# A decoder layer's MLP: up- and down-projection weights fetched, summed and split one k pair at a time, and further ahead

## The chip, the cores and the metric

One core of a Trainium2 chip runs the whole layer in one launch. The metric is device time in microseconds (us). TensorE (PE) multiplies, VectorE (DVE), ScalarE (ACT) and GpSimd (POOL) do element-wise work, SyncE (SP) issues DMAs. Each engine takes its instructions in order, in the order that the kernel's scheduler has written out.

## The reference, cut to what matters

The layer is a hybrid decoder block on 1024 tokens of width 1024: three kinds of attention, gates, an output projection, and then the MLP, which is what the change touches:

```python
h2 = rms_norm(x, norm_mlp_g[l])
x = x + jnp.square(jax.nn.relu(h2 @ w_up[l])) @ w_down[l]      # 1024 -> 4096 -> 1024, float32
```

## The kernel before

Float32 products are made from halves: an operand is split into a rounded `hi` and a remainder `lo` (`split`, ScalarE copies at L90, VectorE subtracts at L91), and each product is three matmuls (`mm3`, L75): hi hi, hi lo, lo hi. The MLP's two big products use a seven-product scheme for 2 x 2 blocks (`PROD`): seven products of sums of blocks instead of eight of blocks. So each step of one k pair (two blocks of 128 along the contraction) is 7 x 3 = 21 matmuls of 128x512, and each run of the loop collects seven PSUM banks, `p0` to `p6`, out of eight. The next run's second product needs a bank of the run before, so evacuation has to follow at once.

**Up-projection (`wino`, 64 steps).** The input `xo` (four k pairs, X0 to X3) stays in SBUF. Runs go over 16 groups of columns, u = 0 to 15, four steps each, but the first group is cut in two, because its last two inputs aren't there yet: u0 with k pairs 0 and 1, u1 whole, u0 with k pairs 2 and 3, then u2 to u15. Per pair of k pairs, `wino_w` has one DMA of 512 KB (SP) into one of two buffers, four GpSimd instructions of 128x256 (`wino_s`, L1105 to L1108) that make the sums of blocks, and then per k pair one split into one of four `wo` buffers. `ahead()` calls it once per step, before the step's matmuls. When a run ends, the banks are combined into four tiles `u2, c11, u3, c21` (L1173 to L1180: one copy on ScalarE, seven adds on VectorE). `use_up` multiplies these by the norm (L1323, VectorE), takes relu and square (L1324, L1325, ScalarE), and makes the sums of blocks for the next product (`wino_t`, L1085 to L1088, `xts`, three on VectorE and one on GpSimd). Squares and sums are stored to DRAM as `r_d` by two DMAs on SP (L1327, L1328).

The norm's own statistics are worked out in between (`rstd`, called through `first`: a few small matmuls `px`, and copies such as L1348).

**Down-projection (64 steps, 16 passes of four).** Pass p makes column group p mod 4 from input k pairs q = p to p + 3. X[q] is loaded from `r_d` (`xload`, L1406, in two pieces, one of four buffers in three), split, and its buffer is used again by X[q + 4], which can load when the last reader of X[q] is done. Weights come per k pair (`wload`, L1413, 256 KB, four GpSimd instructions of 128x128, three `wo` buffers). After a pass the seven banks are added to accumulators (L1457 by ScalarE, L1459 by VectorE); in the first four passes x itself is loaded into some of these first (L1451, L1452). The last passes write the output (L1476 on).

What stands first in each engine's queue is set by a scheduler that works on these loops in program order, with priorities of its own; where `pinned` is set the matmuls' order is as written.

Of the kernel before, what the change touches and what calls it, by code (L numbers as in the profile page):

```python
# [10 lines left out]
F32 = mybir.dt.float32  # L11
# [6 lines left out]
P = 128  # L18
# [13 lines left out]
def f32(ap):  # L32
    return ap.bitcast(F32)
# [22 lines left out]

class Layer:
    def __init__(self, tc, a, out):
        self.tc, self.nc, self.a, self.out = tc, tc.nc, a, out
        self.n = 0  # L60
# [22 lines left out]
    def po_tile(self):  # L83
        return self.ptp.tile([P, 512], F32, tag="tp", name=self.name("po"))

# [995 lines left out]
    def wino_t(self, b):  # L1081

        V, G = self.nc.vector, self.nc.gpsimd
# [4 lines left out]
        V.tensor_sub(t[:, 3], b[:, 3], t[:, 1])  # L1088
# [11 lines left out]
    nwr = nwo = -1  # L1100
# [9 lines left out]
    def wino_w(self, src, kp):  # L1110

        nc = self.nc
        if kp % 2 == 0:
            self.nwr += 1
            self.wraw = self.wrp[self.nwr % 2].tile([P, 2, 8, P], F32, tag="wraw", name=self.name("wraw"))
            nc.sync.dma_start(self.wraw[:, :, 0:4], src[:, kp : kp + 2])
            r = self.wraw
            self.wino_s(r.rearrange("p k q n -> p q k n"))
        r = self.wraw[:, kp % 2]
        self.nwo += 1  # L1120
        wo = self.wop[self.nwo % 4].tile([P, 7, 2, P], F32R, tag="wo", name=self.name("wo"))
        self.split(wo[:, :, 0], wo[:, :, 1], r[:, 1:8])
        return wo

    def wino(self, ws, load, use, first, parts):


        nc = self.nc
        V = nc.vector
# [3 lines left out]
        plan = iter([(u, kp) for u, kps in runs for kp in kps])  # L1133
        W, X = {}, {}

        def ahead():
            n = next(plan, None)
            if n is not None:
                W[n] = self.wino_w(ws[n[0]], n[1])

        ahead()
        for kp in range(3):
            X[kp] = self.wino_x(kp, load)
            if kp == 0:
                ahead()
        for r, (u, kps) in enumerate(runs):
            bank = lambda j: f"p{(7 * r + j + 4) % 8}"
            ps = [self.pw.tile([P, 512], F32, tag=bank(j), name=self.name(f"p{j}")) for j in range(7)]
            for kp in kps:
                ahead()  # L1150
                if (r, kp) == (1, 0):
                    X[3] = self.wino_x(3, load)
                w, x = W[u, kp], X[kp]
                for j, (l, q) in enumerate(self.PROD):
                    self.mm3(ps[j], (w[:, l, 0], w[:, l, 1]), (x[:, q, 0], x[:, q, 1]), kp == kps[0], kp == kps[-1])
                    if (r, kp, j) in ((0, 1, 1), (1, 1, 6), (1, 2, 6), (1, 3, 3)):
                        first(bank(7))
            if r == 0:
                part = parts()
                for t, m in zip(part, ps):  # L1160
                    nc.scalar.copy(t, m)
                continue
            tl = lambda n: self.ev.tile([P, 512], F32, tag=n, name=self.name(n))
            u2, c11, u3, c21 = (tl(n) for n in ("u2", "c11", "u3", "c21"))
            if r == 2:
                for t, m in zip(part, ps):
                    V.tensor_add(t, t, m)
                m1, m2, m6, m7, m4, m5, m3 = part
                V.tensor_add(c11, m1, m2)
                V.tensor_add(u2, m1, m6)  # L1170
            else:
                m1, m2, m6, m7, m4, m5, m3 = ps
                nc.scalar.copy(u2, m1)  # L1173
                V.tensor_add(c11, u2, m2)
                V.tensor_add(u2, u2, m6)  # L1175
            V.tensor_add(u3, u2, m7)
            V.tensor_add(c21, u3, m4)
            V.tensor_add(u3, u3, m5)
            V.tensor_add(u2, u2, m5)
            V.tensor_add(u2, u2, m3)  # L1180
            use(u, (u2, c11, u3, c21))
        self.nwino = len(runs)
        self.pinned = False
# [35 lines left out]
    def tail(self):  # L1219
# [11 lines left out]
        with ExitStack() as c0:  # L1231
# [67 lines left out]
            with ExitStack() as c1:  # L1299
                E = lambda *x, **k: c1.enter_context(tc.tile_pool(*x, **k))  # L1300
                one_ = lambda n: E(name=n, bufs=1)
                xo2, xo3, wrp2, self.ev, wop1, self.xtp, self.xrp, xo0, xo1, wrp1 = (
                    one_(n) for n in ("xo2", "xo3", "wrp2", "ev", "wop1", "xtp", "xrp", "xo0", "xo1", "wrp1")
# [3 lines left out]
                self.wrp, self.wop = (wrp1, wrp2), (wop1, *wop2)  # L1307
# [10 lines left out]
                def use_up(u, cs):  # L1318

                    b = self.xrp.tile([P, 4, 512], F32, tag="xr", name=self.name("rq"))  # L1320
                    for i in (1, 3, 2, 0):
                        hf = i % 2
                        V.tensor_mul(cs[i], cs[i], rb[:, hf * 512 : (hf + 1) * 512])  # L1323
                        nc.scalar.activation(cs[i], cs[i], AF.Relu)  # L1324
                        nc.scalar.activation(b[:, i], cs[i], AF.Square)  # L1325
                    t = self.wino_t(b)
                    nc.sync.dma_start(self.rd[u, :, 0:3], b[:, 1:4])  # L1327
                    nc.sync.dma_start(self.rd[u, :, 3:7], t)  # L1328

# [34 lines left out]
    def down(self):  # L1364
# [4 lines left out]
        with ExitStack() as c1:  # L1369
# [30 lines left out]
            def xload(q):  # L1400

                out = []
                for pool, i, n in xp[q % 4]:
                    t = pool.tile([P, n, 2, 512], F32R, tag=f"x{i}", name=self.name("xd"))
                    raw = f32(t[:, :, 1])
                    nc.sync.dma_start(raw, self.rd[kp(q), :, i : i + n])  # L1406
                    self.split(t[:, :, 0], t[:, :, 1], raw)
                    out += [(t[:, j, 0], t[:, j, 1]) for j in range(n)]
                return out

            def wload(g, kp):
                r = wr.tile([P, 8, P], F32, tag="wraw", name=self.name("wraw"))
                nc.sync.dma_start(r[:, 0:4], a["wdown"][g][:, kp])  # L1413
                self.wino_s(r)
                w = wo.tile([P, 7, 2, P], F32R, tag="wo", name=self.name("wo"))
                self.split(w[:, :, 0], w[:, :, 1], r[:, 1:8])
                return [(w[:, j, 0], w[:, j, 1]) for j in range(7)]

            self.pinned = True
            X = {}  # L1420
            passes = [(p % 4, tuple(range(p, 4 + p))) for p in range(16)]
            last = len(passes) - 1

            W = {}
            plan = iter([(p, q) for p, (g, qs) in enumerate(passes) for q in qs])

            def ahead():
                n = next(plan, None)
                if n is not None:
                    W[n] = wload(n[0] % 4, kp(n[1]))  # L1430

            ahead()
            ahead()
            for p, (g, qs) in enumerate(passes):
                A = acc[g]
                ps = [
# [3 lines left out]
                for run in (qs[0:1], qs[1:2], qs[2:4]) if p == last else [(q,) for q in qs]:  # L1440
                    for q in run:
                        if q not in X:
                            X[q] = xload(q)
                        ahead()
                    for j, (l, x) in enumerate(self.PROD):
                        for q in run:
                            self.mm3(ps[j], W[p, q][l], X[q][x], q == qs[0], q == qs[-1])
                if p < 4:
# [5 lines left out]
                if p <= last - 4:  # L1454
                    for j in range(7):
                        if p < 4 and j in (0, 2, 3):
                            nc.scalar.copy(A[j], ps[j])  # L1457
                        else:
                            V.tensor_add(A[j], A[j], ps[j])  # L1459
                    if p == last - 4:  # L1460
# [13 lines left out]
                if p < last:  # L1474
                    for j in range(7):
                        add(A[j], A[j], ps[j])  # L1476
                    add(a2, a2, a1)
# [10 lines left out]
                else:  # L1488

                    m1, m2, m6, m7, m4, m5, m3 = ps  # L1490
                    nc.scalar.copy(a1, m1)
# [166 lines left out]
```

## Time and profile before

| | us |
|---|---|
| median of 3 runs | 2282.09 (2279.72 to 2284.4) |
| the profiled execution | 2282.35, its span 2280.5 |
| up-projection, first matmul (`p<-xo,wo`) | 1639.42 |
| down-projection, first matmul (`p<-xd,wo`) | 1958.73 |
| last matmul row's start, 37 matmuls | 2267.78 |
| PE, DVE, ACT, POOL busy in the whole span | 96%, 60%, 44%, 21% |
| mean granted TensorE clock | 0.992 |

Times in the profile are microseconds from the span's start. A row of an engine's timeline has start, duration, engine, line, operation, `out<-in`, shape and count; in square brackets is the time for which the engine was idle ahead of it, and who ended that. A slice row has its window, its length, the busy time of PE, PEld (weight loads), DVE, ACT and POOL with the count of instructions in it, the granted TensorE clock, the DMA engines' share and GB/s. A group row has busy time and mean nanoseconds of one instruction, then idle time ahead of it.

### The profile page before, as it was taken

To read this page: it belongs to the slowest core of one execution; us is meant where nothing else is said; L and a number is where in the kernel's file an instruction comes from. 1 tells how busy PE (TensorE), PEld (TensorE's weight loads), DVE (VectorE), ACT (ScalarE), POOL (GpSimd) and SP (SyncE) were. 2 spreads that over 40 slices of the span, in tenths; PEclk is the share of its full clock that TensorE was granted. 3 is DMA by queue.
4 is the path that set the end of the run, shared out by engine and by line. 5 is a ranking of instruction groups with operands and counts; after the bars stand their busy time and mean duration, and the time that the engine had idled before them with its cause. 6 is when DMAs were issued, how large, how long until landed. Compare 5 with 4: busy or idle time off the path is not lost.

```text
span 2280.5 us, 30318 instructions
## 1 busy us (share of the span) xinstructions
PE 2193.9 (96%) x11222; PEld 1878.6 (82%) x11222; DVE 1376.1 (60%) x2627; ACT 1011.8 (44%) x1994; POOL 482.9 (21%) x568
## 2 busy tenths in 40 slices
PE   7999899999999999999898999999999999999999
PEld 5788789887899899999787888887777888778887
DVE  6635457552147877777662124453588777966678
ACT  6533445543246666666553102223444444543332
POOL 2100000000011101111000002101444444665553
PEclk9999999999999999999999999999999999999999
DMA  6023212201321110111135225434644444754444
GB/s 243 24 80 98 86 45 80 84 28 56 98 65 33 38 29 22 31 38 33 33 115 174 91 96 180 134 106 162 203 133 163 152 153 153 280 189 146 151 157 167
DMA packets 113268, 247.89 MB, mean 109 GB/s; under 512 B 10553, under 2 KB 19038, under 8 KB 111070
## 3 DMA queue, kind: packets, MB, share of 16 engines
q1 hardware_dynamic: 113118, 245.94, 32.8%
q8 instruction: 88, 1.44, 0.3%
q14 instruction: 62, 0.51, 0.1%
HBM read 178.76 MB, written 67.14 MB: 108 GB/s over the span
## 4 chain that ended last, share of the span: by engine, by line
PE 70%; DVE 12%; DMA 8%; ACT 5%; issue 3%; POOL 1%; SPq 0%; DVEq 0%; ACTq 0%; POOLq 0%
PE mm L75 41%; PE p L75 19%; PE sc L75 5%; PE po L75 2%; PE tp L78 2%; DMA raw<-in_wd 1%; DVE w L91 1%; ACT dpe L966 1%; DMA xd<-r_d 1%; DVE sc L958 1%; DMA raw<-in_wgate 1%; DVE wo L91 1%; DVE dpe L979 1%; PE pr L78 1%; DVE daT L91 1%
## 5 line engine op out<-in xcount | busy, mean ns | idle before, releaser
L75 PE MATMUL mm<-w,hT 128*128 128x384 f32 (+3 forms) x2496 | 474.2, 331 | 13.8 <-DVE dq L846 9.1
L75 PE MATMUL mm<-hT,w 128*128 128x512 f32 x1920 | 466.9, 397 | 10.7 <-ACT w L90 8.0
L75 PEld LDWEIGHTS mm<-hT,w 128*128 128x128 f32 x1920 | 355.8, 189 | 87.5 <-ACT w L90 9.9
L75 PEld LDWEIGHTS mm<-w,hT 128*128 128x128 f32 x2496 | 387.4, 189 | 33.7 <-DVE dq L846 13.8
L75 PE MATMUL p<-xd,wo 128*128 128x512 f32 x1344 | 309.7, 392 | 8.0 <-DVE xd L91 5.2
L75 PE MATMUL p<-xo,wo 128*128 128x512 f32 x1344 | 308.9, 391 | 6.0 <-DVE u L1175 3.2
L75 PEld LDWEIGHTS p<-xd,wo 128*128 128x128 f32 x1344 | 254.1, 189 | 63.5 <-DVE xd L91 6.4
L75 PEld LDWEIGHTS p<-xo,wo 128*128 128x128 f32 x1344 | 252.4, 189 | 61.1 <-DVE u L1175 3.9
L91 DVE TENSOR_TENSOR w<-raw,w 128x256 fp32r<-128x256 f32 (+3 forms) x304 | 172.7, 589 | 165.4 <-ACT w L90 164.6
L75 PE MATMUL mm<-kt,w 128*128 128x512 f32 x1152 | 261.6, 389 | 0.4 <-DVE w L91 0.4
L75 PEld LDWEIGHTS mm<-kt,w 128*128 128x128 f32 x1152 | 216.1, 188 | 45.6 <-DVE w L91 0.8
L90 ACT CAST w<-raw 128x256 fp32r<-128x256 f32 (+3 forms) x304 | 154.1, 532 | 200.5 <-PE mm L75 110.5
L90 ACT CAST wo<-wraw 128x896 fp32r<-128x896 f32 x128 | 120.2, 941 | 222.1 <-POOL wraw L1108 104.3
L91 DVE TENSOR_TENSOR wo<-wraw,wo 128x896 fp32r<-128x896 f32 x128 | 147.4, 1155 | 82.4 <-ACT wo L90 82.3
L966 ACT ACTIVATE dpe<-sc,dst,drr 128x256 f32<-128x256 f32 (+7 forms) x128 | 106.8, 834 | 93.7 <-DVE dst L962 91.7
L1105 POOL TENSOR_TENSOR wraw<-wraw 128x128 f32<-128x128 f32 (+1 forms) x96 | 74.9, 780 | 219.2 <-DMA wraw<-in_wdown 110.3
L91 DVE TENSOR_TENSOR xd<-xd 128x1536 fp32r<-128x1536 f32 (+2 forms) x43 | 81.8, 1910 | 56.4 <-ACT xd L90 56.3
L958 DVE CUSTOM_DVE_ANT_0 sc<-sc,tmask 128x256 f32<-128x256 f32 (+7 forms) x128 | 97.0, 757 | 16.3 <-PE sc L75 16.3
L1108 POOL TENSOR_TENSOR wraw<-wraw 128x128 f32<-128x128 f32 (+1 forms) x96 | 90.9, 947 | 7.5
L90 ACT CAST xd<-xd 128x1536 fp32r<-128x1536 f32 (+2 forms) x43 | 65.0, 1519 | 60.2 <-DMA xd<-r_d 60.2
L106 POOL TENSOR_SCALAR drr<-drr 128x16 f32<-128x16 f32 x16 | 3.5, 220 | 397.8 <-DVE drr L914 397.8
L75 PE MATMUL mm<-mh,w 128*128 128x512 f32 x256 | 80.6, 395 | 3.8 <-DVE w L91 3.0
(312 smaller groups left out, 2970.9 us busy)
## 6 DMA issues: line engine op xcount, KB each, us to landing
wraw<-in_wup SPq DMA_DIRECT2D x32, 512.0 KB, 4.7
r_d<-xts SPq DMA_DIRECT2D x16, 1024.0 KB, 4.9
wraw<-in_wdown SPq DMA_DIRECT2D x64, 256.0 KB, 2.8
xd<-r_d SPq DMA_DIRECT2D x19, 768.0 KB, 6.1
xd<-r_d SPq DMA_DIRECT2D x14, 1024.0 KB, 5.4
raw<-in_wgate SPq DMA_DIRECT2D x48, 256.0 KB, 3.0
gates<-gt SPq DMA_DIRECT2D x48, 256.0 KB, 2.0
raw<-in_wd SPq DMA_DIRECT2D x32, 384.0 KB, 3.2
```

The costliest lines, as they stand in the source:

```text
L75: self.pin(self.nc.tensor.matmul(out, l, r, start=start, stop=stop))
L78: self.pin(self.nc.tensor.transpose(out, x, self.ident))
L90: nc.scalar.copy(hi, src)
L91: nc.vector.tensor_sub(lo, src, f32(hi))
L106: g.tensor_scalar(r, ss, 1.0 / width, EPS, op0=ALU.mult, op1=ALU.add)
L958: V.tensor_tensor_reduce(out=sc[:, 0:n], in0=sc[:, 0:n], in1=self.tmask[:, D - n : D], scale=1.0, scalar=-3.0e38, op0=ALU.add, op1=ALU.max ...
L966: nc.scalar.activation(pe[c][:, 0:n], sc[:, 0:n], AF.Exp, bias=t8[:, 2 + c : 3 + c], scale=rr[:, i, c : c + 1], accum_out=t8[:, 4 + c : 5 ...
L979: V.scalar_tensor_tensor(out=pe[0][:, 0:n], in0=pe[1][:, 0:n], scalar=t8[:, 7:8], in1=pe[0][:, 0:n], op0=ALU.mult, op1=ALU.add)
L1105: G.tensor_add(r[:, 4], r[:, 0], r[:, 3])
L1108: G.tensor_sub(r[:, 7], r[:, 2], r[:, 5])
```

## The change

- A shared helper `wino_steps` takes the place of `wino_w` and `wload`: per k pair one DMA of 256 KB into the next of its raw buffers (four in the up-projection, in the memory of the two pairs; three in the down-projection, as before) and four GpSimd sums of 128x128. `raw()` issues load and sums of the next k pair, `wsp(n)` splits the weight of a later step (three steps on in the up-projection, two in the down-projection) after step n's matmuls, and then calls `raw()`. The numbers of `wo` buffers stay.
- In the up-projection the first group's partial results are combined in place, and its relu, squares and sums are spread over later steps by generators (`whole`, `todo`). `use_up` is a generator too: squares first, `xts` a step later.
- The store of the squares (`r_d` 0:3) is issued by ScalarE's queue.
- In the down-projection, loads and splits of X are apart: `xdma(q)` after the last step that reads the buffer, `xsplit` of the first piece three steps ahead of first use and of the others two. `side(n)` does this after every step.
- `self.V` and `self.A` are VectorE and ScalarE themselves; the class `InOrder` is added and not used.

By instruction counts, GpSimd has 128 more (573 to 701), SP issues 32 more loads and 16 fewer stores, ScalarE issues 16 DMAs more; TensorE's and VectorE's counts are those of before.

```diff
+    def split2(self, hi, lo, src):
+
+        self.A.copy(hi, src)
+        self.V.tensor_sub(lo, src, f32(hi))
...
-    def wino_w(self, src, kp):
-
-        nc = self.nc
-        if kp % 2 == 0:
-            self.nwr += 1
-            self.wraw = self.wrp[self.nwr % 2].tile([P, 2, 8, P], F32, tag="wraw", name=self.name("wraw"))
-            nc.sync.dma_start(self.wraw[:, :, 0:4], src[:, kp : kp + 2])
-            r = self.wraw
-            self.wino_s(r.rearrange("p k q n -> p q k n"))
-        r = self.wraw[:, kp % 2]
-        self.nwo += 1
-        wo = self.wop[self.nwo % 4].tile([P, 7, 2, P], F32R, tag="wo", name=self.name("wo"))
-        self.split(wo[:, :, 0], wo[:, :, 1], r[:, 1:8])
-        return wo
+    def wino_steps(self, srcs, wrp, wop, lead):
+        raws, W = [], []
+
+        def raw():
+            n = len(raws)
+            if n < len(srcs):
+                r = wrp.tile([P, 8, P], F32, tag="wraw", name=self.name("wraw"))
+                self.nc.sync.dma_start(r[:, 0:4], srcs[n])
+                self.wino_s(r)
+                raws.append(r)
+
+        def wsp(n, split=self.split2, more=True):
+            m = len(W)
+            if m < len(srcs) and m <= n + lead:
+                wo = wop.tile([P, 7, 2, P], F32R, tag="wo", name=self.name("wo"))
+                split(wo[:, :, 0], wo[:, :, 1], raws[m][:, 1:8])
+                W.append(wo)
+            if more:
+                raw()
+
+        return raw, wsp, W
...
+        raw, wsp, W = self.wino_steps([ws[u][:, kp] for u, kps in runs for kp in kps], self.wrp, self.wop, 3)
...
+                if kp != kps[-1]:
+                    wsp(n)
+                    for f in todo.pop(n, []):
+                        next(f)
+            if r == 0:
+                part = parts()
+                for t, m in zip(part, ps):
+                    A.copy(t, m)
+                wsp(n)
+            elif r == 2:
+                for t, m in zip(part, ps):
+                    V.tensor_add(t, t, m)
+                wsp(n)
+
+                def whole():
+                    c = combine(part, False)
+                    yield
+                    yield from use(0, c)
+
+                next(late)
+                g = whole()
+                todo.update({n + 1: [late], n + 3: [g], n + 5: [g], n + 8: [g]})
+            else:
+                cs = combine(ps, True)
+                wsp(n)
+                g = use(u, cs)
...
                     for i in (1, 3, 2, 0):
                         hf = i % 2
-                        V.tensor_mul(cs[i], cs[i], rb[:, hf * 512 : (hf + 1) * 512])
-                        nc.scalar.activation(cs[i], cs[i], AF.Relu)
-                        nc.scalar.activation(b[:, i], cs[i], AF.Square)
-                    t = self.wino_t(b)
-                    nc.sync.dma_start(self.rd[u, :, 0:3], b[:, 1:4])
+                        self.V.tensor_mul(cs[i], cs[i], rb[:, hf * 512 : (hf + 1) * 512])
+                        self.A.activation(cs[i], cs[i], AF.Relu)
+                        self.A.activation(b[:, i], cs[i], AF.Square)
+                    self.A.dma_start(self.rd[u, :, 0:3], b[:, 1:4])
+                    yield
+                    t = self.wino_t(b, self.V)
                     nc.sync.dma_start(self.rd[u, :, 3:7], t)
+                    yield
...
+            raw, wsp, W = self.wino_steps([a["wdown"][g][:, kp(q)] for g, q in steps], wr, wo, 2)
...
+            def side(n):
+
+                wsp(n)
+                for q in use1:
+                    if q >= 4 and use9[q - 4] == n:
+                        xdma(q)
+                for q in use1:
+                    if q >= 3 and n == use1[q] - 3:
+                        xsplit(q, (0,))
+                    if q >= 3 and n == use1[q] - 2:
+                        xsplit(q, (1, 2))
```

More of the change, by code (lines that the diff above doesn't have):

```diff
@@ L1098, in wino_x @@
         return xo
-    nwr = nwo = -1
     def wino_s(self, r):
@@ L1125, in wino @@
     def wino(self, ws, load, use, first, parts):
-        nc = self.nc
-        V = nc.vector
+        V, A = self.V, self.A
         self.pinned = True
         runs = [(0, (0, 1)), (1, (0, 1, 2, 3)), (0, (2, 3))] + [(u, (0, 1, 2, 3)) for u in range(2, len(ws))]
[L1133 to L1175, printed above, removed]
@@ L1403, in xload, with xdma @@
+            def xdma(q):
+                X[q] = []
                 for pool, i, n in xp[q % 4]:
                     t = pool.tile([P, n, 2, 512], F32R, tag=f"x{i}", name=self.name("xd"))
[L1405 to L1433, printed above, removed]
+                    nc.sync.dma_start(f32(t[:, :, 1]), self.rd[kp(q), :, i : i + n])
```

124 lines of the change are left out of this document (105 added, 19 removed).

## The prediction

> **What bounds the kernel now.** I read the page first, then the slices of 10 us over the two stages that the change touches, TensorE's timeline in them, and the rows around each hole. The slices' sum (busy time from 1640 to 2280 us, mean in tenths) says which engine to watch:
>
> ```profile
> sum 640.00, PE 620.94 PEld 509.55 DVE 483.30 ACT 277.82 POOL 325.80; mean PE 9.70 PEld 7.96 DVE 7.55 ACT 4.34 POOL 5.09
> ```
>
> TensorE is busy 97% of it, so the change can only win back holes, or dig new ones. The change keeps every matmul. TensorE's timeline (start, duration, count, idle before and its releaser):
>
> ```profile
> 1652.53 14.53 PE L75 MATMUL p<-xo,wo 128*128 128x512 f32 x63 [1.58 <-ACT pt L1161]
> ...
> 1672.20 1.16 PE L75 MATMUL px<-dg,ones 128*128 128x128 f32 x8 [1.51 <-ACT rb L1348]
> ...
> 1709.21 22.00 PE L75 MATMUL p<-xo,wo 128*128 128x512 f32 x87 [3.18 <-DVE u L1175]
> 1734.06 224.83 PE L75 MATMUL p<-xo,wo 128*128 128x512 f32 x990 [0.43 <-DVE u L1179]
> 1958.73 6.86 PE L75 MATMUL p<-xd,wo 128*128 128x512 f32 x28
> 1967.65 5.05 PE L75 MATMUL p<-xd,wo 128*128 128x512 f32 x21 [2.06 <-DVE xd L91]
> 1975.87 49.48 PE L75 MATMUL p<-xd,wo 128*128 128x512 f32 x209 [3.16 <-DVE xd L91]
> 2027.18 239.70 PE L75 MATMUL p<-xd,wo 128*128 128x512 f32 x1049 [1.83 <-DVE acc L1459]
> ```
>
> Undisturbed, a matmul takes 224.83 / 990 = 0.2271 us, so one step (21 matmuls) 4.77 us and one run or pass of four steps 19.1 us. All holes lie in the first 95 us of the up-projection and the first 70 us of the down-projection. The slices (busy time and count of PE, PEld, DVE, ACT, POOL, then the clock) give each hole's whole price, with the slowed matmuls after it:
>
> ```profile
> 1670.00:1680.00 10.00, 8.49 (x42) 6.86 (x41) 7.64 (x11) 5.46 (x9) 4.39 (x5) 1.00 0.10 37
> ...
> 1700.00:1710.00 10.00, 6.82 (x30) 5.16 (x28) 7.42 (x9) 1.73 (x3) 8.92 (x9) 1.00 0.94 330
> 1710.00:1720.00 10.00, 9.86 (x37) 7.88 (x37) 8.47 (x12) 8.58 (x13) 1.50 (x2) 0.83 0.50 143
> ...
> 1730.00:1740.00 10.00, 8.90 (x37) 6.40 (x36) 9.02 (x13) 6.54 (x11) 5.04 (x5) 1.00 0.29 90
> ...
> 1970.00:1980.00 10.00, 6.84 (x23) 5.17 (x23) 10.00 (x8) 4.40 (x4) 9.46 (x7) 0.83 0.68 247
> ```
>
> A slice without a hole counts about 45 (44 that start in it, and edges). After the 3.18 us hole the granted clock is 0.83 for a slice, with 37 matmuls. Against 45, the slices from 1700 and 1710 lack 15 + 8 = 23 matmuls, 23 x 0.2271 = 5.2 us; the one from 1730 lacks 8, 1.8 us; the hole at 1672 is 1.5 us by its own row.
>
> **Why those holes are there.** The rows at the largest one, oldest first (a DMA from the chain of waits, then the engines' timelines), those at the other two, and the wait's total (us, times, longest):
>
> ```profile
> 1697.94 4.45 DMA wraw<-in_wup
> 1706.20 0.94 ACT L90 CAST wo<-wraw 128x896 fp32r<-128x896 f32 x1 [5.61 <-POOL wraw L1108]
> 1707.17 1.39 DVE L91 TENSOR_TENSOR wo<-wraw,wo 128x896 fp32r<-128x896 f32 x1 [2.51 <-ACT wo L90]
> 1708.48 0.67 DVE L1175 TENSOR_TENSOR u<-u,p 128x512 f32<-128x512 f32 x1
> 1726.74 0.94 ACT L90 CAST wo<-wraw 128x896 fp32r<-128x896 f32 x1 [6.17 <-POOL wraw L1108]
> 1670.72 0.94 ACT L90 CAST wo<-wraw 128x896 fp32r<-128x896 f32 x1 [7.35 <-POOL wraw L1108]
> ACT wo L90 <- POOL wraw L1108: 95.8, 25, 7.4
> ```
>
> A raw weight pair lands at 1702.4, GpSimd's sums (L1108 is the last) hold it further, ScalarE waits 5.61 us with the split of that weight at the head of its queue, VectorE waits behind it, and the evacuation of the finished banks (L1175) stands behind that split in VectorE's order. TensorE needs the bank. The other two holes have the same row in front, 6.17 and 7.35 us of ScalarE waiting for L1108; at 1672 it is the broadcast copy L1348 that queues behind it.
>
> **Part 1, raws per k pair.** The price of a load and of its sums (landing; GpSimd rows with count, busy and mean ns; the pair's form first):
>
> ```profile
> wraw<-in_wup SPq DMA_DIRECT2D x32, 512.0 KB, 4.7
> wraw<-in_wdown SPq DMA_DIRECT2D x64, 256.0 KB, 2.8
> L1105 POOL TENSOR_TENSOR wraw<-wraw 128x256 f32<-128x256 f32 x30 | 31.7, 1056 | 68.7 <-DMA wraw<-in_wup 56.9 <-DVE xts L1088 9.0 <-DVE c L1174 2.7
> L1107 POOL TENSOR_TENSOR wraw<-wraw 128x256 f32<-128x256 f32 x30 | 28.9, 962 | 0.0
> L1106 POOL TENSOR_TENSOR wraw<-wraw 128x256 f32<-128x256 f32 x30 | 25.6, 855 | 0.0
> L1108 POOL TENSOR_TENSOR wraw<-wraw 128x256 f32<-128x256 f32 x30 | 24.1, 802 | 2.4
> L1105 POOL TENSOR_TENSOR wraw<-wraw 128x128 f32<-128x128 f32 x64 | 41.5, 648 | 126.3 <-DMA wraw<-in_wdown 110.3 <-DVE wo L91 15.9
> L1107 POOL TENSOR_TENSOR wraw<-wraw 128x128 f32<-128x128 f32 x64 | 35.5, 555 | 0.0
> L1106 POOL TENSOR_TENSOR wraw<-wraw 128x128 f32<-128x128 f32 x64 | 46.6, 728 | 0.0
> L1108 POOL TENSOR_TENSOR wraw<-wraw 128x128 f32<-128x128 f32 x64 | 65.4, 1021 | 5.0
> ```
>
> Before, a pair's buffer is free when the split of the pair two back is done, and its own first split comes three steps later: 3 x 4.77 = 14.3 us, of which load (4.7) and sums (1.06 + 0.96 + 0.86 + 0.80 = 3.68) take 8.4. That leaves 5.9 us on paper, and any bunching of splits, or another DMA ahead in SP's queue, eats it. After, each of four slots is free four steps before its next split: 19.1 us, less 2.8 for the same 256 KB as in the down-projection and 0.65 + 0.56 + 0.73 + 1.02 = 2.95 for sums of that shape: 13.3 us of slack. SP's queue still holds raws behind the first loads of xd, whose 4.84 us is seen in this row; 13.3 - 4.8 is still 8.5:
>
> ```profile
> 1704.55 4.84 SPq L1406 DMA_DIRECT2D xd<-r_d  x2
> ```
>
> So the split heads no queue with its raw missing, and the three holes go: 1.5 + 5.2 + 1.8 = 8.5 us. I keep 0.5 of the last one, since VectorE is 90% busy in its slice as it is, and the spread of the first row's result now lands there: -8.0. From the other side, the bound is the part that is surely a raw's wait, 3.18 + 1.51 = 4.7; on the far side -10, with the hole of 1.58 us at 1652. That one I leave: its two raws are still issued there. In the order of the changed kernel ScalarE and VectorE are not pinned by the new helper class, which nothing instantiates; the order that the scheduler gives has the same evacuation, behind a split, in every steady run.
>
> What it adds: 32 more DMA issues on SP, and 128 more GpSimd instructions. GpSimd's sums in the up-projection go from 30 x 3.68 = 110 to 62 x 2.95 = 183 us of about 320; still under 60% of them, cost 0. But they run beside VectorE:
>
> ```profile
> 1960.37 0.46 POOL L1105 TENSOR_TENSOR wraw<-wraw 128x128 f32<-128x128 f32 x1 [6.43 <-DMA wraw<-in_wdown]
> 1974.06 2.08 POOL L1105 TENSOR_TENSOR wraw<-wraw 128x128 f32<-128x128 f32 x1 [0.38 <-DMA wraw<-in_wdown]
> 1972.47 3.35 DVE L91 TENSOR_TENSOR xd<-xd 128x2048 fp32r<-128x2048 f32 x1
> ```
>
> The same sum takes 0.46 us with VectorE out of the way and 2.08 us while VectorE splits a wide tile. The Trainium skill, "SBUF - State Buffer", section Who interferes with whom, says that GpSimd shares one port pair with VectorE under an exclusive lock; these rows agree, and by that rule more GpSimd instructions mean more chances to hold VectorE up, which speaks against the change. Priced from rows: if each of the 64 weight splits is held by one more free-running sum, 64 x 0.46 = 29 us of VectorE, 1.8 per run, against a VectorE that is 75.5% busy by the sum (4.7 us free per run): 0 on the path, except in the runs that are already full, where it is up to 2 x 1.8 = +3.6. I take 0 and put 3.6 in the range.
>
> **Part 2, squares stored from ScalarE's queue.** Sixteen issues move from SP. An SP issue takes 0.42 us in this row; if ScalarE pays the same, 0.42 per run of 19.1 us:
>
> ```profile
> 1698.41 0.42 SPq L1327 DMA_DIRECT2D r_d<-rq  x1
> ```
>
> ScalarE is about half idle, so 0; if its copies wait behind an issue, at most 16 x 0.42 = +6.7 spread over runs whose evacuations have slack, of which I count +1 as the outer bound. What SP gains is nothing that a wait showed.
>
> **Part 3, the change of stage, 1958 to 1986.** VectorE is the bound there (10.00 busy in the slice above); its work is not made less. X1's and X2's wide splits ended the two TensorE holes of 2.06 and 3.16 us. What moves: X0's last third loads earlier, and X4's split goes ahead of the evacuation of the first pass:
>
> ```profile
> 1977.87 4.48 DVE L91 TENSOR_TENSOR xd<-xd 128x1536 fp32r<-128x1536 f32 x2
> ```
>
> Replaying the new order by hand with durations of these rows (T = 1958.7): the first step loses about 2.9 us, one evacuation behind X1's wide split and one behind a weight split; the later two holes shrink by as much, and step 3 ends at about T + 25 where it was T + 28. X4's three pieces (about 4.2 us of VectorE) then stand before the evacuation, and step 4 ends at T + 32.5, as now. Net 0. The ends are -4 and +4: the two holes with half of their slow matmuls (the slice from 1970 lacks 22 matmuls, 5.0 us) won, or X4's 4.2 us of VectorE fully in TensorE's way.
>
> Further on the same pattern exists already, the hole of 1.83 at 2027:
>
> ```profile
> 2009.06 7.87 DMA xd<-r_d
> 2018.90 2.29 DVE L91 TENSOR_TENSOR xd<-xd 128x2048 fp32r<-128x2048 f32 x1 [6.51 <-ACT xd L90]
> ```
>
> X6 is loaded when X2's last reader is done, takes 7.87 us, and its split stands before pass 2's evacuation. After, X5 stands so before pass 1's as well, and X6's group holds two VectorE instructions less: +1 and -1, with 0 to +3 and -2 to 0. From pass 4 on, order and waits are those of before: 0.
>
> **Sum.** -8.0 + 0 + 0 + 0 = -8.0 on the profiled execution's 2282.35 us, 2274.3; that one lies 0.26 above the median of the three, so **2274**.
>
> **The rivals.**
> (a) *The first passes hold the evacuation.* X4, X5 and X6 each stand before an evacuation, and if each load is late as X6's is now, each costs what that hole costs, 1.83 idle and, by the count of 31 in its slice, about 14 matmuls or 3.3 us in all:
>
> ```profile
> 2020.00:2030.00 10.00, 8.17 (x31) 6.36 (x30) 9.92 (x10) 4.72 (x6) 9.12 (x10) 0.87 0.19 55
> ```
>
> Three times with a full second split (2.0 to 2.3 us) behind it is 3 x 5.5 = 16.5, less the 3.3 already paid: +13, and with -8 above it 2287, slower. It decides from the point where an X load lands more than about 12 us after the previous use of its buffer ends (three steps, 14.3 us, less 2.3). For it: X4's loads share the queues with the last stores. Against: X5 is loaded in the same way now, and the row of 209 matmuls from 1975.87 to 2025 has no hole in it.
> (b) *The holes of the up-projection stay half.* VectorE, 74 to 90% busy in the slices from 1700 to 1740 although it waits there, is the next bound, and the late raw only hid it: holes merge into one behind VectorE, -3 to -4 remains; with +3 from (a) in small: 2281, no change.
> (c) *Both clear.* The early loads also take the 2.06 and 3.16 us holes and their slow clock (of the 5.0 us that the slice from 1970 lacks, and the 2.06): 2274 - 7 = 2267. The Trainium skill, "TensorE: Matmul & The Clock Gate", Part 1, says that an idle window of about 3.4 us brings the clock down; the trace shows 0.83 after 3.18 us, and a shortened hole would by that rule win more than its own length. Against: VectorE's 30 busy us there are not less.
>
> **Chances.** Forecast (-5 to -11) 0.45, (c) 0.13, (b) 0.17, (a) 0.25. A measurement of this kernel can tell about 0.2%, 4.6 us, from no change. Faster by more than that: the forecast and (c), 0.58, less a little for its edge, 0.57; same: (b), 0.18; slower: (a), 0.25. The range runs from (c)'s 2267 less 3 for the outer bound of the stage change, 2264, to (a)'s 2287; the forecast's own range is 2271 to 2277.
>
> **What would show it.** In the new profile: ScalarE's wait for L1108 (95.8 us now in the MLP) falls below 40; no TensorE hole over 1 us between 1670 and 1740; clock 1.00 in those slices; sums of 128x128 only. Right for part 3: holes in the first 30 us of the down-projection that sum to about what they are now (5.2 us idle). Wrong: a TensorE wait for an evacuation (acc) after the first or second pass of over 3 us, or ScalarE's queue waiting at its new DMA issues with copies of banks behind it.

## The result, and the profile after

The changed kernel is slower: 2287.9 us median (2285.01 to 2289.55, 7 runs) against 2282.09 (2279.49 to 2284.4, 7 runs), ratio 1.0025, 95% interval 1.0015 to 1.0035. I had forecast 2274, a gain; it is a loss of 0.25%, a small one that is clear of the noise. The profiled execution took 2289.55 us, its span is 2287.7, 7.2 longer than before's 2280.5.

TensorE's timeline of the changed kernel, rows after a hole (start, duration, count, idle before and its releaser; line numbers are now the changed kernel's, L91 is the matmul, L1543 the evacuation of the down-projection, L105 a split):

```profile
1653.22 14.56 PE L91 MATMUL p<-xo,wo 128*128 128x512 f32 x63 [1.77 <-DVE st L1397]
...
1707.60 18.51 PE L91 MATMUL p<-xo,wo 128*128 128x512 f32 x78 [0.42 <-DVE u L1184]
1726.58 1.75 PE L91 MATMUL p<-xo,wo 128*128 128x512 f32 x6 [0.48 <-DVE u L1181]
1728.76 224.70 PE L91 MATMUL p<-xo,wo 128*128 128x512 f32 x990 [0.43 <-DVE u L1184]
1953.30 3.56 PE L91 MATMUL p<-xd,wo 128*128 128x512 f32 x15
1958.54 0.96 PE L91 MATMUL p<-xd,wo 128*128 128x512 f32 x3 [1.68 <-DVE c L1182]
1961.55 14.97 PE L91 MATMUL p<-xd,wo 128*128 128x512 f32 x52 [2.05 <-DVE u L1184]
...
1988.34 132.12 PE L91 MATMUL p<-xd,wo 128*128 128x512 f32 x573 [1.58 <-DVE acc L1543]
2120.93 20.41 PE L91 MATMUL p<-xd,wo 128*128 128x512 f32 x87 [0.47 <-DVE acc L1543]
2143.41 37.68 PE L91 MATMUL p<-xd,wo 128*128 128x512 f32 x165 [2.07 <-DVE acc L1543]
2182.96 19.39 PE L91 MATMUL p<-xd,wo 128*128 128x512 f32 x84 [1.87 <-DVE acc L1543]
2202.87 20.08 PE L91 MATMUL p<-xd,wo 128*128 128x512 f32 x87 [0.53 <-DVE acc L1543]
2224.04 18.65 PE L91 MATMUL p<-xd,wo 128*128 128x512 f32 x81 [1.09 <-DVE acc L1561]
2243.73 0.97 PE L91 MATMUL p<-xd,wo 128*128 128x512 f32 x3 [1.04 <-DVE acc L1561]
2245.49 28.65 PE L91 MATMUL p<-xd,wo 128*128 128x512 f32 x125 [0.80 <-DVE acc L1561]
```

The up-projection did what was forecast. The hole of 1.51 us is gone, the one of 3.18 is down to 0.42, and the stage takes 1953.30 - 1639.92 = 313.4 us where it took 319.3. That is one execution of each: in the nine other profiles with this up-projection it takes 312.7 to 316.7 us, in the one other profile with the old one 318.4, so a gain of some 4 to 6 us is as much as can be said. The down-projection has new holes, those from 2120 to 2246 all released by an evacuation, in a stretch that had none. To see all of it, I take the time from the first matmul of a pass to the first of the next, as the single matmuls' starts in the trace give it, and subtract 0.2271 us for each matmul (in the up-projection the small matmuls `px` as well):

| us lost | up | pass 0 | 1 | 2 | 3 | 4-7 | 8-9 | 10-11 | 12-13 | 14-15 | down |
|---|---|---|---|---|---|---|---|---|---|---|---|
| before | 10.2 | 7.9 | 0.0 | 0.0 | 3.7 | -0.2 | -0.1 | -0.1 | 0.0 | 1.3 | 12.5 |
| changed | 4.3 | 7.6 | 5.9 | 0.0 | 0.0 | 0.3 | 3.4 | 2.1 | 2.2 | 3.7 | 25.1 |

Won 5.9, lost 12.6 and another 0.5 before the first of these stages: 7.2 together. Of the 12.6, passes 0 to 3 hold 1.9 and passes 4 to 15 hold 10.8.

One cycle of the late holes, in the order in which the changed kernel's engines took it (VectorE, SP's queue, ScalarE, VectorE; `xd 128x2048` is the wide piece of the next X; the row of 2166.12 is the last two loads of the row of 2159.00):

```profile
2160.83 4.26 DVE L1543 TENSOR_TENSOR acc<-acc,p 128x512 f32<-128x512 f32 x7
2165.01 3.27 DVE L105 TENSOR_TENSOR wo<-wraw,wo 128x896 fp32r<-128x896 f32 x3
2159.00 8.45 SPq L1138 DMA_DIRECT2D wraw<-in_wdown  x3
2166.12 1.33 SPq L1138 DMA_DIRECT2D wraw<-in_wdown  x2
2167.50 0.97 SPq L1476 DMA_DIRECT2D xd<-r_d  x2
2174.86 1.91 ACT L104 CAST xd<-xd 128x2048 fp32r<-128x2048 f32 x1 [7.70 <-DMA xd<-r_d]
2176.80 2.29 DVE L105 TENSOR_TENSOR xd<-xd 128x2048 fp32r<-128x2048 f32 x1 [8.52 <-ACT xd L104]
2182.23 4.26 DVE L1543 TENSOR_TENSOR acc<-acc,p 128x512 f32<-128x512 f32 x7
```

And a cycle of the kernel before, three passes earlier:

```profile
2102.76 4.26 DVE L1459 TENSOR_TENSOR acc<-acc,p 128x512 f32<-128x512 f32 x7
2106.94 1.08 DVE L91 TENSOR_TENSOR wo<-wraw,wo 128x896 fp32r<-128x896 f32 x1
2108.42 0.43 SPq L1406 DMA_DIRECT2D xd<-r_d  x1
2113.69 1.91 ACT L90 CAST xd<-xd 128x2048 fp32r<-128x2048 f32 x1 [4.04 <-DMA xd<-r_d]
2121.09 1.08 DVE L91 TENSOR_TENSOR wo<-wraw,wo 128x896 fp32r<-128x896 f32 x1
2122.09 4.26 DVE L1459 TENSOR_TENSOR acc<-acc,p 128x512 f32<-128x512 f32 x7
```

It is a loop, once round in each pass. An evacuation delays a weight split behind it; that split frees a raw buffer; a raw load waits for that buffer at the head of SP's queue; X's load stands behind the raw load; X's split waits for X; and X's split stands ahead of the next evacuation in VectorE's order. TensorE gives such a loop 19.1 us. Before: from evacuation to X's issue 5.7 us, to its landing 5.3, to the next evacuation 8.4, in all 19.3. A sum close to the pass proves nothing by itself, since steady evacuations are a pass apart in any case. What shows that the loop was near its limit is that nothing in it waits for TensorE: the evacuations of 2102.76 and 2122.09 follow VectorE's splits without idle time. By the starts in the trace, the evacuations ahead of passes 6 to 12 begin only 0.2 to 1.0 us before TensorE's first matmul of that pass (3.0 once). A TensorE without holes did not show that.

After: 6.7, since the raw load ahead of X now waits for the second weight split behind the evacuation, then 7.4 to the landing, then 7.4 (one weight split less in front): 21.4 here, and 19.9 with the median landing of the wide piece, 5.9 us. The first and the last leg together are 14.1 us, as before. So by these rows all of the difference is X's later landing. Why it lands later isn't shown. Two raw loads and X's other piece are issued within 2 us of it in these rows, where before it was one raw load; but X's pieces side by side are not enough, since two runs below that issue them so have a median of 5.3 (side work first, and X held).

The old down-projection shows the same sensitivity. In the run with the store back on SP (below), which has it unchanged, one wide piece took 7.4 us to land, with its other piece 2 us behind it, and one hole came of it:

```profile
2072.50 4.26 DVE L1519 TENSOR_TENSOR acc<-acc,p 128x512 f32<-128x512 f32 x7
2078.18 0.58 SPq L1466 DMA_DIRECT2D xd<-r_d  x1
2085.56 1.91 ACT L111 CAST xd<-xd 128x2048 fp32r<-128x2048 f32 x1 [6.90 <-DMA xd<-r_d]
2093.66 4.26 DVE L1519 TENSOR_TENSOR acc<-acc,p 128x512 f32<-128x512 f32 x7
2094.39 135.18 PE L91 MATMUL p<-xd,wo 128*128 128x512 f32 x588 [1.79 <-DVE acc L1519]
```

There no other hole follows for 588 matmuls, seven passes; in the changed kernel six of the seven passes from 8 to 14 have one.

### The profile page after: what moved, and what is told of

The parts are those of the page before. It is cut to its first block, busy times and chain, and to the rows that moved or that the text cites. A ratio compares the mean times of both kernels' runs of the same rounds, so it can differ in the third digit from the quotient of the medians.

```text
span 2287.7 us, 30578 instructions
## 1 busy us (share of the span) xinstructions
PE 2203.0 (96%) x11222; PEld 1884.3 (82%) x11222; DVE 1388.2 (61%) x2627; ACT 1012.3 (44%) x1994; POOL 543.9 (24%) x696
## 4 chain that ended last, share of the span: by engine, by line
PE 70%; DVE 14%; DMA 7%; ACT 5%; issue 3%; POOL 2%; SPq 0%; ACTq 0%; DVEq 0%; POOLq 0%
PE mm L91 43%; PE p L91 18%; PE sc L91 4%; ACT dpe L987 2%; PE po L91 2%; DVE sc L979 1%; PE tp L94 1%; DMA wraw<-in_wdown 1%; DMA raw<-in_wd 1%; DVE wo L105 1%; DVE w L112 1%; DVE dpe L1000 1%; DVE daT L112 1%; DVE dq L867 1%; DMA raw<-in_wgate 1%
## 5 line engine op out<-in xcount | busy, mean ns | idle before, releaser
L91 PE MATMUL mm<-w,hT 128*128 128x384 f32 (+3 forms) x2496 | 474.0, 331 | 13.7 <-DVE dq L867 9.0
L91 PE MATMUL mm<-hT,w 128*128 128x512 f32 x1920 | 471.0, 400 | 8.2 <-ACT w L111 5.2
L91 PEld LDWEIGHTS mm<-hT,w 128*128 128x128 f32 x1920 | 360.1, 191 | 84.9 <-ACT w L111 5.8
L91 PEld LDWEIGHTS mm<-w,hT 128*128 128x128 f32 x2496 | 387.4, 189 | 33.3 <-DVE dq L867 13.7
L91 PE MATMUL p<-xd,wo 128*128 128x512 f32 x1344 | 314.1, 395 | 16.2 <-DVE acc L1543 8.5
L91 PEld LDWEIGHTS p<-xd,wo 128*128 128x128 f32 x1344 | 253.9, 190 | 76.3 <-DVE acc L1543 12.4
L91 PE MATMUL p<-xo,wo 128*128 128x512 f32 x1344 | 307.5, 390 | 3.2 <-DVE st L1397 1.8
L91 PEld LDWEIGHTS p<-xo,wo 128*128 128x128 f32 x1344 | 251.4, 188 | 57.9 <-ACT pt L1210 2.2
L91 PE MATMUL mm<-kt,w 128*128 128x512 f32 x1152 | 261.3, 389 | 0.0
L91 PEld LDWEIGHTS mm<-kt,w 128*128 128x128 f32 x1152 | 216.2, 188 | 45.0 <-DVE w L112 0.2
L104 ACT CAST wo<-wraw 128x896 fp32r<-128x896 f32 x122 | 114.8, 942 | 187.7 <-PE p L91 121.9
L105 DVE TENSOR_TENSOR wo<-wraw,wo 128x896 fp32r<-128x896 f32 x122 | 146.2, 1213 | 51.3 <-ACT wo L104 51.1
L1124 POOL TENSOR_TENSOR wraw<-wraw 128x128 f32<-128x128 f32 x128 | 100.9, 788 | 207.3 <-DMA wraw<-in_wdown 132.5
L105 DVE TENSOR_TENSOR xd<-xd 128x1536 fp32r<-128x1536 f32 (+2 forms) x36 | 69.2, 1929 | 69.4 <-ACT xd L104 69.3
L1125 POOL TENSOR_TENSOR wraw<-wraw 128x128 f32<-128x128 f32 x128 | 100.9, 788 | 0.0
L1126 POOL TENSOR_TENSOR wraw<-wraw 128x128 f32<-128x128 f32 x128 | 90.7, 708 | 0.0
```

Source lines behind the costliest of these rows:

```text
L91: self.pin(self.nc.tensor.matmul(out, l, r, start=start, stop=stop))
L104: self.A.copy(hi, src)
L105: self.V.tensor_sub(lo, src, f32(hi))
L1124: G.tensor_add(r[:, 4], r[:, 0], r[:, 3])
L1125: G.tensor_sub(r[:, 5], r[:, 4], r[:, 1])
L1126: G.tensor_sub(r[:, 6], r[:, 1], r[:, 0])
```

## The experiments

All ratios are against the kernel before on the same chip. The theories carry the names of the expectations.

**The halves apart.** The changed up-projection over the old down-projection, and the reverse.

> The up-projection as changed, with the down-projection of the kernel before. In the changed profile the up-projection is 5.9 us shorter (313.4 for 319.3 us between first matmuls) and the down-projection 12.6 us longer. Theory A (the loss is made in the down-projection alone, by weight splits that now stand behind the evacuation): 2282 - 6 = 2276 us, faster by 0.25%, with the down-projection back at about 309 us to its last row. Theory B (the same, by X loads ahead of the raws in SP's queue): also 2276. Theory C (the up-projection's doubled GpSimd work or the store on ScalarE's queue costs something that shows only later): 2282 or more.

> The down-projection as changed, with the up-projection of the kernel before. A and B: 2282 + 10 to 13 = 2292 to 2295 us, with holes ahead of the passes after the eighth as in the changed kernel. C: 2284 or less. If the two halves add up, this and the one with the up-projection alone sum to the changed kernel's +5.8.

Measured: 2274.7 us, ratio 0.9976 (0.9964 to 0.9989), and 2294.1, ratio 1.0056 (1.0038 to 1.0075). The halves' ratios add to +0.32%, the whole measured +0.25%. With the old down-projection TensorE's last 1002 matmuls have no hole:

```profile
2041.25 227.46 PE L91 MATMUL p<-xd,wo 128*128 128x512 f32 x1002 [0.42 <-DVE acc L1519]
```

So the up-projection's gain is real and the loss is made in the down-projection alone: C falls. (The profiled execution of the reverse took 2286.3 us, the fastest of its six.)

**The place of the weight split.** The changed kernel's down-projection splits the weight of step n + 2 after step n. The old one did so before step n, which is one step earlier: its last split of a pass stood ahead of the evacuation. Two edits give that order of splits back:

```diff
-            raw, wsp, W = self.wino_steps([...], wr, wo, 2)
+            raw, wsp, W = self.wino_steps([...], wr, wo, 3)
```

> The changed kernel with the down-projection's weight split three steps ahead in place of two (same buffers). Then the split of the next weight stands ahead of the evacuation again in VectorE's order, as before. A: the eight or nine us of holes in passes 8 to 14 go, 2287.9 - 8.5 = 2279 us. B: SP's queue still has both pieces of X ahead of the raws, so the holes stay: 2287 us.

```diff
                 if p <= last - 4:
+                    side(n)
                     for j in range(7):
...
-                    side(n)
```

> The changed kernel with the side work of a pass's last step (next weight's split, raw load, X's load and split) written ahead of the evacuation in place of behind it; lead of two as changed. VectorE's order in passes 8 to 14 becomes that of before, as with a lead of three. A: 2279 us as with the lead of three, by another edit. B: 2287 us.

Measured: 2295.0 us, ratio 1.0063 (1.0047 to 1.008), and 2288.3, 1.0039 (1.0025 to 1.0053). A falls: neither is faster than the changed kernel in all, and the lead of three makes it worse (34.7 us lost in its profile's down-projection). A split ahead of the evacuation frees the raw buffer earlier but is itself ahead of the evacuation; it shifts about 1 us from one leg of the loop to the other (with the side work first 5.7 and 8.6 us, in the changed kernel 6.7 and 7.4). With the side work first, where the wide piece lands in 5.3 us at the median, passes 4 to 15 lost 7.2 us in place of 11.7, and passes 0 to 3 lost 2.2 more.

**Program order on VectorE and ScalarE.** The class `InOrder` used in the down-projection, and in both:

```diff
+            self.V, self.A = InOrder(tc, nc.vector), InOrder(tc, nc.scalar)
             V, A_ = self.V, self.A
```

> The changed kernel, with VectorE's and ScalarE's instructions of the down-projection held in program order by the helper class that the change adds and doesn't use. Then X's split is no longer hoisted ahead of an evacuation: it stands behind it, a pass after its load was issued. The run with a lead of three had the old order of weight splits and was slower (2295), so the lead alone isn't the cause. Theory D (what makes the late holes is X's split standing ahead of the evacuation in VectorE's queue while its data still travels; the changed SP order makes it land later): holes of passes 8 to 14 go, as do those of the first passes behind X4: 2287.9 - 10 to 12 = 2276 to 2278. Theory B (raws behind X's load in SP's queue): raws still are, 2287.

> The same with the up-projection's VectorE and ScalarE instructions held in program order too. D: as the run before in the down-projection; in the up-projection the evacuation then stands ahead of the next split, so the last 4.3 us lost there can go: 2272 to 2278. B: 2287 or so.

Measured: 2274.2 us, ratio 0.9958 (0.9943 to 0.9972), the lowest of all (its interval overlaps that of the changed up-projection over the old down-projection), and 2291.7, 1.0039 (1.0027 to 1.0052). Held in order, X's split stands behind the evacuation, a pass after its load, and the down-projection has not one hole in its last 1254 of 1344 matmuls (TensorE, VectorE):

```profile
1985.12 284.65 PE L91 MATMUL p<-xd,wo 128*128 128x512 f32 x1254 [1.63 <-DVE acc L67]
```

```profile
2094.25 4.77 DVE L67 TENSOR_TENSOR acc<-acc,p 128x512 f32<-128x512 f32 x7 [3.33 <-PE p L91]
2098.94 2.09 DVE L67 TENSOR_TENSOR wo<-wraw,wo 128x896 fp32r<-128x896 f32 x2
2100.95 1.75 DVE L67 TENSOR_TENSOR xd<-xd 128x1536 fp32r<-128x1536 f32 x1
```

VectorE now waits 3.33 us for TensorE ahead of the evacuation, not the other way round; the evacuation starts 3.9 us ahead of TensorE's next pass. In the up-projection the same edit loses: it takes 331.5 us, and in the rows ScalarE then keeps weight splits behind the squares, the first group's and a later one's (holes of 4.33 and 3.88 us, released by ScalarE's split). I had expected a gain there; the scheduler's order is the better one in that stage.

**Which of the held instructions mattered.** X's splits and evacuations held, weights free; and the reverse.

> The changed kernel with only X's splits and the evacuations of the down-projection held in program order among themselves; the weight splits are left to the scheduler. Each X split stands behind the evacuation again, a pass after its load. D (X's split ahead of the evacuation is the cause): no holes in passes 2 to 14, 2274 to 2277 us, like the run with all of it held. A' (it is the place of the weight splits that the holding mended): holes stay, 2284 to 2288.

> The mirror of the run before: weight splits and evacuations held in program order, X's splits left to the scheduler, which puts them ahead of the evacuation as in the changed kernel, with three weight splits right behind the evacuation. D: holes as in the changed kernel, 2285 to 2290 us. A': no holes, 2274 to 2277.

Measured: 2280.9 us, ratio 0.9992 (0.998 to 1.0003), and 2294.5, 1.0053 (1.0038 to 1.0068). TensorE with X held, then two rows of the one with the weights held:

```profile
1987.53 287.33 PE L91 MATMUL p<-xd,wo 128*128 128x512 f32 x1254 [7.38 <-DVE acc L67]
```

```profile
2181.18 19.39 PE L91 MATMUL p<-xd,wo 128*128 128x512 f32 x84 [2.02 <-DVE acc L67]
2253.67 19.38 PE L91 MATMUL p<-xd,wo 128*128 128x512 f32 x84 [2.58 <-DVE wo L67]
```

With X held the late holes are gone, so they need X's split ahead of the evacuation, as D says; A' falls. (That the split's place alone doesn't make them, the next runs show.) My 2274 to 2277 was missed all the same: the scheduler put three weight splits and one of X's pieces ahead of the first evacuations, which made one hole of 7.38 us, early in pass 1. Weights and X have to be held together there.

**Why the loop got longer.** The SP queue of the down-projection held in program order, with X's pieces one raw load apart (as before the change) or together:

```diff
+            self.S = InOrder(tc, nc.sync)
...
-                    nc.sync.dma_start(f32(t[:, :, 1]), self.rd[kp(q), :, i : i + n])
+                    self.S.dma_start(f32(t[:, :, 1]), self.rd[kp(q), :, i : i + n])
```

> The changed kernel, VectorE and ScalarE left to the scheduler (X's split ahead of the evacuation), but with the down-projection's SP queue held in program order and X's 3x512 piece loaded one step after the others, so that a raw load lies between the pieces as in the kernel before. Theory E (X's split stands ahead of the evacuation before and after; what broke is that both pieces are now issued within 1 us and the wide one lands later): the holes of passes 8 to 14 shrink to 2 us or less in all, 2278 to 2281. Theory F (the bunched weight splits behind the evacuation keep the holes alive without it): 2285 to 2289.

> The control: SP's queue held in program order too, but both pieces of X issued together as in the changed kernel. E and F: holes as in the changed kernel or worse, 2286 to 2293. If it is as fast as the run with the gap, holding SP's order was what mattered, not the gap.

Measured: 2288.6 us, ratio 1.0033 (1.002 to 1.0046), and 2290.4, 1.0037 (1.0027 to 1.0048). The totals say F, the profiles do not: both lose nothing in passes 2 to 13, with three weight splits between the evacuation and the next X as in the changed kernel. They lose it elsewhere, 17 us in passes 0 and 1 and 5 to 8 in the last two.

```profile
1989.03 268.41 PE L91 MATMUL p<-xd,wo 128*128 128x512 f32 x1172 [3.22 <-DVE acc L1552]
```

So the bunch alone keeps no hole alive, nor does X's split ahead of the evacuation, and the gap between the pieces is not needed: E falls as I put it. In both, X's load stands one raw load earlier in SP's queue than in the changed kernel, and is issued 4.3 to 5.5 us after the start of passes 4 to 12, where the changed kernel drifts from 3.6 in pass 4 to 8.6 in passes 9 and 11. The last run moves X's load back behind that one raw load:

```diff
-                    if q >= 4 and use9[q - 4] == n:
+                    if q >= 4 and use9[q - 4] == n - 1:
                         xdma(q)
```

> The run with SP held in program order and X's pieces together (no holes in passes 4 to 12, X's loads behind raw loads 13, 17, 21 and so on), with X's load written one step later, so that one raw load more stands ahead of it in SP's queue (14, 18, 22, as in the changed kernel). VectorE's order in passes 4 to 12 is the same in both. Theory G (that raw load waits for its slot, which a weight split behind the evacuation frees; so a late evacuation makes the next X late, and with X's split ahead of the next evacuation the delay feeds itself): passes of 20 to 21 us again, 8 us or more lost in passes 4 to 12, 2296 us or more. Theory H (one raw load more is nothing; holding SP in order, or the place of the 3x512 piece, was what helped): 0.3 us lost per two passes, 2288 to 2291.

Measured: 2289.3 us, ratio 1.0026 (1.0012 to 1.004). H's pattern, no hole, holds for passes 2 to 10:

```profile
1990.22 207.40 PE L91 MATMUL p<-xd,wo 128*128 128x512 f32 x912 [0.18 <-DVE acc L1544]
2198.47 19.38 PE L91 MATMUL p<-xd,wo 128*128 128x512 f32 x84 [0.85 <-DVE acc L1544]
2218.07 20.10 PE L91 MATMUL p<-xd,wo 128*128 128x512 f32 x87 [0.22 <-DVE acc L1562]
2238.88 20.01 PE L91 MATMUL p<-xd,wo 128*128 128x512 f32 x84 [0.71 <-DVE acc L1562]
```

Then X's issue drifts: 5.0 us after the start of passes 2 to 9, but 5.7, 6.8 and 8.8 in passes 10, 11 and 12, and holes come in every pass, as in the changed kernel. So the raw load ahead of X does not cost by itself: it stands there for eight passes without a hole. In this run the wide piece is split last, so its landing is 4.2 us from the evacuation (7.4 in the changed kernel); three evacuations in a row, from 2157 on, start 20.2 us apart. Neither G nor H as worded. That the holes need the loop is shown by the runs that take X's split out of it. What tipped it from 19.3 to 19.9 and 21.4, the raw load ahead of X, the landing or SP's order, is argued from the rows and stays open.

**Parts of the up-projection.** On the changed up-projection over the old down-projection: the store back on SP, and two raw buffers in place of four.

> The up-projection as changed over the down-projection of before (2274.7), with the store of the squares issued by SP again. If the store's move is worth nothing, as I priced it: 2274 to 2276. If it is what frees SP for the raws: 2279 or more.

> The up-projection as changed over the down-projection of before (2274.7), with two raw buffers of one k pair in place of four: each k pair is still fetched and summed by itself, but only 2 x 4.77 = 9.5 us ahead, of which load and sums took 5.75. If being further ahead is what removed the three holes: they come back in part, 2278 to 2284 us. If the finer piece alone does it: 2274 to 2276.

Measured: 2279.6 us, ratio 0.9984 (0.9971 to 0.9997), beside 0.9976 (0.9964 to 0.9989) with the store on ScalarE. The time lies where I had put "the move frees SP", but the kernel before was 1.8 us slower beside this run (2281.7 for 2279.9) and the intervals overlap: the store's move is worth at most about 0.3%, none is shown, and none is ruled out.

With two buffers 2338.6 us, 1.023 (1.0211 to 1.025): far beyond the 2284 that I had as the worst. ScalarE's waits for the sums in the up-projection: before, then the changed kernel (three rows), then two buffers:

```profile
ACT wo L90 <- POOL wraw L1108: 80.4, 16, 7.4
```

```profile
ACT wo L104 <- POOL wraw L1125: 3.8, 1, 3.8
ACT wo L111 <- POOL wraw L1127: 3.8, 1, 3.8
ACT wo L104 <- POOL wraw L1127: 2.3, 2, 1.6
```

```profile
ACT wo L104 <- POOL wraw L1127: 104.9, 27, 4.8
```

So the distance matters: half the buffer memory, and with it half the way ahead, loses 2.5% over four buffers. Two buffers of one k pair are also less than the kernel before had, two of two k pairs, so what the finer piece does by itself, at the old distance, wasn't run.

## Why the prediction was wrong, point by point

- *Three holes of the up-projection go, -8.0.* Right in kind and by the mechanism that was named: ScalarE's wait for the sums in that stage falls from 80.4 to 9.9 us (3.8 + 3.8 + 2.3, shown above). The size is 5.9 in the profiled execution. The hole at 1672 went, and that of 3.18 us shrank to 0.42. What I left for the last, 0.5, was too little: two holes of 0.48 and 0.43 us by VectorE's combine remain, and their slice lacks nine matmuls, 2.0 us:

```profile
1720.00:1730.00 10.00, 8.96 (x36) 6.16 (x35) 9.65 (x13) 2.63 (x4) 7.62 (x11) 1.00 0.88 320
```

  VectorE is 97% busy there: this is rival (b) in small.
- *128 more GpSimd instructions, 0 on the path.* Nothing speaks against it: the up-projection that has 128 more of them is the faster one. VectorE's weight splits there did get longer, before and after:

```profile
L91 DVE TENSOR_TENSOR wo<-wraw,wo 128x896 fp32r<-128x896 f32 x64 | 71.7, 1125 | 54.2 <-ACT wo L90 54.1
```

```profile
L105 DVE TENSOR_TENSOR wo<-wraw,wo 128x896 fp32r<-128x896 f32 x61 | 73.8, 1228 | 32.8 <-ACT wo L104 32.8
```

  They take 103 ns more each, 6 us of VectorE over 61 splits, where the bound was 29; VectorE's idle time ahead of them fell from 54.2 to 32.8 us. No run separates GpSimd's part in it. The shared port pair of the Trainium skill ("SBUF - State Buffer", Who interferes with whom) agrees with the direction. The sum of 0.46 us that I took as free of VectorE ran beside a combine on VectorE (`c<-u,p`, 1959.93 to 1960.61), so that row does not show an idle VectorE.
- *The store on ScalarE, 0.* Not decided by what was measured.
- *The change of stage, 0 (-4 to +4).* Passes 0 to 3 lost 1.9 more: inside the range, but by two errors that nearly cancel. Pass 0 lost 7.6 for 7.9. X4's split ahead of the first evacuation cost 5.9 in pass 1, where nothing was lost before; and the hole of 1.83 us, 3.7 with its slow matmuls, went from pass 3, which I had not forecast.
- *"From pass 4 on, order and waits are those of before: 0."* This step failed, and with it the sign: 10.8 us. The order was not that of before: a weight split had gone from ahead of each evacuation to behind it, both pieces of X were issued together, and X's load waited for a later weight split. And I had read no slack there at all. A stretch in which TensorE has no hole looked safe, while its evacuations started as little as 0.2 us ahead of the next pass. The term was put at 0 on a claim that no row backed; the runs show in its place holes of 0.5 to 2.1 us in six of the seven passes from 8 to 14, which go when X's split is held behind the evacuation. Which of the three moves tipped it stays open.
- *Rival (a)* had the mechanism, X's split ahead of an evacuation while its data travels, and its time, 2287; the time is luck. Of its three early passes one paid, with 5.9 us close to the 5.5 that it gave each, and the rest of the loss came in the late passes, of which it says nothing, and through a loop that it doesn't have.
- *What would show it.* ScalarE's wait for the sums was to fall below 40 us over both stages; it fell to 50.3, since the down-projection's part rose. No hole over 1 us is left between 1670 and 1740, as said. The holes in the down-projection's first 30 us sum to 5.1 us idle, for 5.2 before, but 2.3 more follow in the next five. *Wrong* named an evacuation wait of over 3 us after the first or second pass; after the first there are three of 1.24, 0.72 and 1.58, and the late ones are 0.5 to 2.1 us, seven of them, where I was not looking.

## What to carry to other kernels

Where TensorE has no hole, measure the loops behind it all the same: follow one buffer from its last reader through the load, the split and the evacuation to its next reader, and look for the place in it that waits for TensorE. Where none waits, as in the kernel before, a later microsecond becomes a hole, once or, as in the changed kernel, in pass after pass. And a load issued earlier helps only if its consumer stands where the load has time to land: holding the down-projection's VectorE and ScalarE in program order, with X's split behind the evacuation, turned the change from 0.25% slower into 0.42% faster than the kernel before, while the same edit in the up-projection cost more than that.

## What the runs showed of the hardware

The granted clock fell in the changed kernel after holes no longer than 2.05 us:

```profile
1960.00:1970.00 10.00, 8.46 (x24) 6.68 (x25) 10.00 (x11) 10.00 (x11) 5.42 (x7) 0.66 0.89 306
```

In slices of 2 us it is 0.50 from 1962 to 1966 here, and 0.50 from 1710 to 1712 after the 3.18 us hole of the kernel before (0.83 over its 10 us): as deep, but for longer. By the Trainium skill ("TensorE: Matmul & The Clock Gate", Part 1: the clock drops after an idle window of about 3.4 us) single holes of this size would not bring it down. Here two holes of 1.68 and 2.05 us, with three matmuls (0.96 us) between them, did it, and in the kernel before the one hole of 1.83 us at 2027 did (0.50 from 2028 to 2030). After the late holes of 2.07 and 1.87 us, ending at 2143 and 2183, it stayed at 1.00. So the length of a single hole does not decide it here.

Of two loads of X issued about 0.5 us apart the second takes longer to land than where they are issued apart (medians from 2060 to 2262 us). Its piece of 768 KB takes 6.6 to 7.4 us behind the one of 1 MB (seven runs), and 5.1 to 6.1 where it is issued about 2 us or more behind (three runs). With the order turned round, as the scheduler left it in the two runs with SP held and X's pieces together, it takes 4.8 and 5.7, and the piece of 1 MB behind it 6.9 and 8.7. Where the 1 MB is first, no such rule shows: its medians are 5.3 to 6.7 us together and 5.1 to 5.7 apart.
